# Scores in groups of four, one accumulator pair, and a longer queue of filler: the attention of a two-layer diffusion trunk, regrouped

## The chip, the cores and the metric

The kernel runs on the 8 cores of one Trainium2 chip, each core on its own share of tokens, with no exchange between them. The metric is the device time in microseconds (us) of the slowest core. Executions come in two states. In the slow one the cores of one die, or of both, run at a lower granted clock and the time is 6 to 17% longer. A ratio is the mean time of one kernel's fast runs over that of the other's of the same rounds, so it is not quite the ratio of the medians that stand beside it.

## The reference, cut to what matters

```python
# layer 0, per core: 512 context tokens (two prompts of 256) and 1281 latent tokens (1024 of its own and a halo)
h = modulate(x, g, shift, scale)                         # RMSNorm and adaLN
q, k, v, b, c, u = split(h @ w_in)                       # attention and short convolution share it
o_p = softmax([sink | q_p k_p^T / 8]) v_p                # context: 2 key blocks of 128 for each query block
o_s = softmax([sink | band of 3 key blocks | 512 cached context keys]) v    # latent: 7 key blocks
x = x + gate * (concat(o, b * dwconv3(c * u)) @ w_out)   # projection of attention and convolution
x = x + gate2 * conv_ffn(modulate(x, ...))               # then the feed-forward; layer 1 is another mixer
```

8 heads share 2 key/value heads. With 4 heads x 128 queries, one key block gives two score matmuls (one per key/value head) of 64 rows (the head dimension) by 512 columns, one exp over 128 x 1024, and two value matmuls of 512 columns. There are 13 query blocks of 128 and 70 key blocks for them, and one lone query of the halo (neighbours' tokens that a core works out for itself). SP is the prompt; S0, S1 and S2 are the latent pieces of 385, 384 and 384 tokens. A bank is one of the eight parts, 0 to 7, of the memory into which TensorE writes (PSUM). Filler is other TensorE work that is put between the key blocks.

## The kernel before

Python emits operations in program order with their dependencies; a list scheduler with a cost model then fixes each engine's order. TensorE keeps program order unless an operation isn't ready in the model. The parts that matter, cut and shortened:

```python
BK.free = [6, 7]                     # banks for filler; scores use 0, 1
ODs = ((2, 3), (4, 5))               # accumulators: two pairs, alternating by query block

def s_mm(i, u):                      # scores of one key block: two matmuls on upper and lower array half
    for hh in range(2):
        P.mm(bk(hh, 0, 512), kt(u["ky"], hh), qv(u["bl"], hh))
def s_exp(i, u):
    act_pair(pts[i % 3].whole(), 0, pair(0, 0, 512), AF.Exp, 0.125)     # then a mask on VectorE for some
def s_pv(i, u):                      # values and row sums; at a block's end normalise()
    ...
def normalise(bl):                   # 4 VectorE reads of the accumulators, Ln and Exp on ScalarE,
    ...                              # the product on GpSimd

for i in range(len(un) + 2):         # 70 key blocks
    def step(i=i):
        if i >= 2: s_pv(i - 2, un[i - 2])
        if i < len(un): s_mm(i, un[i]); s_exp(i, un[i])
    emit(step)
    acc += rate                      # n_fill / (70 - 6)
    while acc >= 1.0:                # filler: convolution, adaLN, projection of prompt and S0
        acc -= 1.0
        if fill: emit(fill.popleft())
# [cut] the lone query; then the projection of S1 and S2 beside the norm of prompt and S0; then the feed-forward
```

Of the kernel before, what the change touches and what calls it, by code (L numbers as in the profile page):

```python
# [126 lines left out]
class Prog:  # L127
# [93 lines left out]
    def cost(eng, reads, writes, is_dma):  # L221
# [7 lines left out]
        if eng == "pe":  # L229
            m = 1  # L230
            for d in reads[1].ap.shape[1:]:
                m *= d
            return max(27.0, m / 2.4 + 2.6)
# [264 lines left out]
KC = 8  # L498
# [39 lines left out]
def build():  # L538
# [40 lines left out]
    with es:  # L579
# [322 lines left out]
        IN_FLIGHT = 3.4e6  # L902
        seq = []

        def gate(n):
            n *= 512
            for op, m in reversed(seq):
                n += m
                if n > IN_FLIGHT:
                    return [op]  # L910
            return []
# [75 lines left out]
        mxS = P.tile("mxS", [128, KC, NX], BF16, O_W + 8192)  # L987
# [9 lines left out]

        def mx_(st, k):
            return mxP[:, k, :] if st.p else mxS[:, k, st.t0:st.t1]
# [4 lines left out]
        def qk_chunk(st, c):  # L1004
# [14 lines left out]
            def tail():  # L1019
# [12 lines left out]
                else:  # L1032
# [5 lines left out]
                    dst = mxS[:, c, st.t0:st.t1] if c < 4 else kS[:, st.t0:st.t1]  # L1038
# [102 lines left out]

        def norm_now(nm):
            stats(nm)
            for k in range(KC):
                nm.apply(k, E1[k], E2[k])
# [40 lines left out]
        for i in range(3):  # L1186
            pts.append(P.tile(f"pt{i}", [128, 2, 512], BF16, A_PT + 2048 * i))
# [3 lines left out]
        for c in range(4):  # L1191
            release(("q", c))

# [16 lines left out]
        for qb in range(9):  # L1210
# [5 lines left out]
            blocks.append(dict(p=False, q0=qb * 128, nq=128, keys=loc[:-1] + ks + loc[-1:]))  # L1216
        un = []
        for bl in blocks:
            for i, ky in enumerate(bl["keys"]):
                un.append(dict(bl=bl, ky=ky, first=i == 0, last=i == len(bl["keys"]) - 1))  # L1220
        BK.free = [6, 7]
        nblk = [0]
        ODs = ((2, 3), (4, 5))
# [12 lines left out]
        def s_mm(i, u):  # L1236
            for hh in range(2):
                out = bk(hh, 0, 512)
                P.mm(out.v("p (g q) -> p g q", g=4), kt(u["ky"], hh), qv(u["bl"], hh))

# [9 lines left out]
        def s_exp(i, u):  # L1250
            pt = pts[i % 3]
            act_pair(pt.whole(), 0, pair(0, 0, 512), AF.Exp, 0.125)
            mk = u["ky"][4]
            if mk is not None:
                m = tab[:, 128 + 128 * mk:256 + 128 * mk]
                pv = pt.whole().v("p h (g q) -> p (h g) q", g=4)
                P.tt("dve", pv, pv, m.w(m.ap.unsqueeze(1).to_broadcast([128, 8, 128])), ALU.mult)

        def s_pv(i, u):
            pt = pts[i % 3]  # L1260
            vb = u["ky"][3]
            kn = u["ky"][2]
            for hh in range(2):
                P.mm(bk(ODs[nblk[0] % 2][hh], 0, 512), vt[0:kn, vb, 64 * hh:64 * hh + 128], pt[0:kn, hh, :],
                     start=u["first"], stop=u["last"])
            if u["last"]:
                normalise(u["bl"])

        def normalise(bl):
            r = nrm[nblk[0] % len(nrm)]  # L1270
            OD = ODs[nblk[0] % 2]
            nblk[0] += 1
            d, nn = r["d"], r["n"]
# [29 lines left out]
        accs = [P.tile(f"acc{i}", [128, NP], F32, A_RP + 4096 + 2048 * i) for i in range(2)]  # L1303
        nA = [Norm(0, 1, SP, None, None, acc=accs[0]), Norm(0, 1, S0, None, None, acc=accs[1])]

        def oproj_a(st, nm, k):
            assert all(bl.get("done") for bl in blocks[:8])
            oproj_item(0, "we", mx_, st, nm, k, False)

        for k in range(KC):  # L1310
            for st, nm in ((SP, nA[0]), (S0, nA[1])):
                fill.append(lambda st=st, nm=nm, k=k: oproj_a(st, nm, k))
        n_fill = len(fill)
        acc = 0.0
        rate = n_fill / (len(un) - 6.0)
        for i in range(len(un) + 2):
            def step(i=i):
                if i >= 2:
# [477 lines left out]
```

## Time and profile before

| before | value | how to read it |
|---|---|---|
| median time | 1203.85 us | 16 runs, of them the fast ones 1201.9 to 1206.3 |
| PE busy | 94% of the span | TensorE is the bound almost everywhere, but a matmul at half clock is "busy" for longer (two value matmuls 1.03 us there, 0.60 otherwise) |
| first score matmul | 144.4 us | median of the eight cores |
| from it to the first feed-forward matmul | 178.3 us | median of the eight cores |
| half clock in that stretch | 27.3 us | worked out from the trace's clock records |
| from there to the last matmul | 874.5 us | PE saturated for most of it |

The stretches and the timeline are in the prediction below. In these views PE is TensorE, DVE VectorE, ACT ScalarE and POOL GpSimd; `64*128 64x512 bf16 x2` is two matmuls on 64 rows and 128 columns of the array that stream 512 columns each; brackets give the engine's idle time before and what ended it; PEclk is the granted clock. One more view of before, TensorE's waits (core 1; total us, times, longest):

```profile
PE ps L346 <- DVE pt L367: 5.6, 8, 1.1
PE ps L346 <- ACT pt L1246: 5.6, 12, 1.4
PE ps L346 <- DVE modv L367: 1.8, 2, 0.9
```

`pt` are the weights of a key block, which exp makes on ScalarE and some masks change on VectorE. "DVE pt" are value matmuls that wait for a mask. "ACT pt" are mostly score matmuls that wait until exp has read their banks: the view of the tile `pt` puts only 1.0 us of the 5.6, 3 times of 12, ahead of instructions that use `pt`. The three lines add up to 13 us, less than the 16 us for which TensorE is idle in this stretch.

### The profile page before, as it was taken

How to read it: one execution, taken by the hardware profiler on the slowest of the kernel's cores; microseconds unless marked ns; L12 is line 12 of the kernel's file. 1: busy time of each engine (PE TensorE's matmuls, PEld its weight loads, DVE VectorE, ACT ScalarE, POOL GpSimd, SP SyncE). 2: the span in 40 equal slices, each digit the busy share in tenths (PEclk: the TensorE clock that was granted, in tenths of full speed). 3: DMA queues.
4: the chain of work that ended last, by engine and by line, in shares of the span. 5: the costliest groups of instructions: out<-in, count | busy, mean ns of one | idle time of the engine just before them, and what ended most of it. 6: DMA issues, size and time to landing. Idle time of an engine off the chain costs nothing.

```text
span 1202.5 us, 21586 instructions; the slowest of 8 cores (1196.9 to 1202.5 us)
## 1 busy us (share of the span) xinstructions
PE 1129.9 (94%) x7169; PEld 625.2 (52%) x7169; DVE 748.4 (62%) x1264; ACT 622.2 (52%) x1084; POOL 480.2 (40%) x551
## 2 busy tenths in 40 slices
PE   1498999897999999999999999998999999999998
PEld 1245543332555555555555654654556566555566
DVE  3288875554689888888512522646798888882111
ACT  2276576676786555555311546445786666660000
POOL 2146521241574445454332632755764444441000
PEclk9999999997999999999999999999999999999999
DMA  9993353910404587876364570134035322225751
GB/s 178 177 207 50 52 92 52 147 29 1 71 2 73 92 140 120 140 124 124 62 111 86 92 141 1 28 53 71 12 66 101 57 51 50 49 50 116 153 128 56
DMA packets 32605, 102.28 MB, mean 85 GB/s; under 512 B 3312, under 2 KB 10096, under 8 KB 32112
## 3 DMA queue, kind: packets, MB, share of 16 engines
q0 software_dynamic: 23616, 85.21, 42.9%
q1 hardware_dynamic: 8880, 15.69, 4.0%
q8 instruction: 60, 0.98, 0.3%
q14 instruction: 49, 0.40, 0.1%
HBM read 179.27 MB, written 6.82 MB: 155 GB/s over the span
## 4 chain that ended last, share of the span: by engine, by line
PE 84%; DMA 8%; DVE 3%; issue 2%; ACT 2%; POOL 0%; SPq 0%; DVEq 0%; ACTq 0%; POOLq 0%
PE ps L346 84%; DMA xS<-xs 3%; DMA w_ada<-ada 3%; ACT pt L1246 1%; DMA xP<-xp 1%; DMA xT<-xs 1%; DVE nd L367 1%; DVE vn L388 1%; DVE pt L367 0%; DVE cvt L388 0%; ACT hS L362 0%; ACT rrs L362 0%; DVE tg L367 0%; DVE nn L394 0%; DVE xS L388 0%
## 5 line engine op out<-in xcount | busy, mean ns | idle before, releaser
L388 DVE SCALAR_TENSOR_TENSOR ft<-ps,cf,ft 128x510 f32<-128x510 f32 (+5 forms) x704 | 417.4, 630 | 67.8 <-ACT ft L362 32.9
L346 PE MATMUL ps<-hS,w_up 128*128 128x386 bf16 (+4 forms) x2112 | 334.9, 318 | 0.0
L362 ACT ACTIVATE ft<-ps,cf 128x384 f32<-128x384 f32 (+4 forms) x354 | 208.8, 592 | 130.9 <-PE ps L346 122.9
L346 PEld LDWEIGHTS ps<-hS,w_up 128*128 128x128 bf16 x2112 | 206.3, 98 | 126.6
L346 PE MATMUL ps<-hP,w_up 128*128 128x512 bf16 x704 | 160.3, 379 | 0.0
L388 DVE SCALAR_TENSOR_TENSOR xS<-ps,modv,xS 128x384 f32<-128x384 f32 (+4 forms) x96 | 56.7, 593 | 141.6 <-PE ps L346 141.0
L367 POOL TENSOR_TENSOR actT_a<-ft,ft 128x512 bf16<-128x512 f32 (+3 forms) x96 | 99.4, 1036 | 108.5 <-DVE ft L388 94.9
L346 PE MATMUL ps<-actT_a,w_dn 128*128 128x384 bf16 (+4 forms) x768 | 140.5, 333 | 0.0
L367 POOL TENSOR_TENSOR actT_b<-ft,ft 128x512 bf16<-128x512 f32 (+2 forms) x80 | 82.8, 1036 | 121.0 <-DVE ft L388 107.3
L362 ACT ACTIVATE ft<-ft 128x384 f32<-128x384 f32 (+4 forms) x178 | 95.6, 537 | 46.0 <-DVE ft L388 41.0
L346 PE MATMUL ps<-actT_b,w_dn 128*128 128x384 bf16 (+4 forms) x640 | 118.9, 333 | 0.0
L346 PEld LDWEIGHTS ps<-hP,w_up 128*128 128x128 bf16 x704 | 67.7, 98 | 75.4 <-issue 0.3
L346 PEld LDWEIGHTS ps<-actT_a,w_dn 128*128 128x128 bf16 x768 | 75.2, 98 | 54.9
L1246 ACT ACTIVATE pt<-ps 128x1024 bf16<-128x1024 f32 (+2 forms) x73 | 71.9, 985 | 35.1 <-PE ps L346 34.5
L346 PEld LDWEIGHTS ps<-actT_b,w_dn 128*128 128x128 bf16 x640 | 62.7, 98 | 45.7
L388 DVE SCALAR_TENSOR_TENSOR xP<-ps,modv,xP 128x512 f32<-128x512 f32 x32 | 24.0, 750 | 93.6 <-PE ps L346 93.5
L362 ACT ACTIVATE hS<-xS 128x384 bf16<-128x384 f32 (+3 forms) x84 | 41.7, 510 | 66.2 <-DVE xS L388 64.5
L346 PE MATMUL ps<-hS,w_cv 128*128 128x386 bf16 (+2 forms) x288 | 59.1, 333 | 4.0 <-DVE cvt L367 1.5
L400 POOL DMA_DIRECT2D w_dn<-w_dn x32 | 18.3, 572 | 103.8 <-PE ps L346 88.6
L346 PE MATMUL ps<-pt,vtok 128*128 128x512 bf16 (+2 forms) x154 | 46.9, 392 | 8.8 <-DVE pt L367 5.6
L346 PE MATMUL ps<-scb,w_ada 128*128 128x2 bf16 x768 | 25.2, 164 | 22.0 <-DMA w_ada<-ada 21.6
L362 ACT ACTIVATE hP<-xP 128x512 bf16<-128x512 f32 x28 | 17.2, 626 | 51.9 <-DVE xP L388 43.7
(183 smaller groups left out, 1337.6 us busy)
## 6 DMA issues: line engine op xcount, KB each, us to landing
w_ada<-ada POOLq DMA_DIRECT2D x48, 512.0 KB, 7.8
w_up<-w_up POOLq DMA_DIRECT2D x44, 512.0 KB, 8.2
w_dn<-w_dn POOLq DMA_DIRECT2D x32, 704.0 KB, 7.1
w_cv<-w_cv POOLq DMA_DIRECT2D x4, 768.0 KB, 9.5
xS<-xs SPq DMA_DIRECT2D x2, 1536.0 KB, 11.3
xP<-xp SPq DMA_DIRECT2D x1, 2048.0 KB, 12.0
w_we<-w_oe POOLq DMA_DIRECT2D x8, 256.0 KB, 5.1
w_u<-w_u POOLq DMA_DIRECT2D x8, 256.0 KB, 4.7
```

The costliest lines, as they stand in the source:

```text
L346: return self.add("pe", lambda e: e.matmul(out.ap, lhsT.ap, rhs.ap, start=start, stop=stop), reads=[lhsT, rhs], writes=[out])
L362: op = self.add("act", lambda e: e.activation(out.ap, in_.ap, func, **kw), reads=reads, writes=writes)
L367: return self.add(eng, lambda e: e.tensor_tensor(out.ap, in0.ap, in1.ap, op), reads=[in0, in1], writes=[out])
L388: return self.add(eng, lambda e: e.scalar_tensor_tensor(out.ap, in0.ap, sc, in1.ap, op0, op1), reads=reads, writes=[out])
L400: op = self.add(q, lambda e: e.dma_start(out.ap, in_.ap), reads=[in_], writes=[out], is_dma=True)
L1246: op = P.add("act", lambda e: e.activation(out.ap, ap, func, scale=scale), reads=r, writes=[out])
```

## The change

Its intent: pay the TensorE's change between 64-row and 128-row matmuls once per two key blocks, fill the attention to its end, and let what follows start earlier. The core of the diff:

```diff
+            if reads[0].ap.shape[0] == 64 and m > 256:     # cost model of a score matmul
+                return m / 4.8 + 53.0
...
         def norm_now(nm):
+            n0 = len(P.ops)
             stats(nm)
+            if prev:                                       # squares wait for the norm ahead
+                for o in P.ops[n0:n0 + KC]:
+                    o.deps.add(prev[-1])
+            prev.append(nm.last.idx)
...
+        blocks = [bl for two in zip(blocks[0:4], blocks[4:8]) for bl in two] + blocks[8:]
+        # steps of two key blocks; after block 7 the lone query (None)
-        ODs = ((2, 3), (4, 5))
+        OD = (4, 5)
...
+            for s, u in enumerate(steps[i]):               # four score matmuls, banks 0 to 3
+                for hh in range(2):
+                    ops.append(P.mm(bk(2 * s + hh, 0, 512) ...))
+            # the first takes over all dependencies, the others follow it at top priority
...
-        nA = [Norm(0, 1, SP, None, None, acc=accs[0]), Norm(0, 1, S0, None, None, acc=accs[1])]
+        nA = [Norm(0, 1, st, tA, rA[i], acc=accs[i]) for i, st in enumerate((SP, S0))]   # own buffers
+        fill.append(lambda: queue_apply(nA))
+        for k in range(KC):
+            fill.append(lambda k=k: oproj_a(S1, nB[0], k, 11))   # S1's projection is filler
+        KEEP = 5
-        rate = n_fill / (len(un) - 6.0)
+        rate = (len(fill) - KEEP) / float(len(steps))
```

More of the change, by code (lines that the diff above doesn't have):

```diff
@@ L900, in build @@
         SP = St(1, 0, NP)
-        IN_FLIGHT = 3.4e6
+        limit = [3.4e6]
         seq = []
@@ L908, in gate @@
                 n += m
-                if n > IN_FLIGHT:
+                if n > limit[0]:
                     return [op]
@@ L986, in build @@
         mxP = P.tile("mxP", [128, KC, NP], BF16, O_W)
-        mxS = P.tile("mxS", [128, KC, NX], BF16, O_W + 8192)
         kP = P.tile("kP", [128, NP], BF16, A_K)
@@ L996, in build @@
         nrm = []
+        ms = [P.tile("mxS", [128, KC, NX], BF16, O_W + 8192)]
         def mx_(st, k):
-            return mxP[:, k, :] if st.p else mxS[:, k, st.t0:st.t1]
+            return mxP[:, k, :] if st.p else ms[0][:, k, st.t0:st.t1]
         cos_, sin_ = (lambda a, b: cs0[:, 0, a:b]), (lambda a, b: cs0[:, 1, a:b])
@@ L1037, in tail @@
                     P.tt("pool", r["t"][:, 0, 0:n], r["t"][:, 0, 0:n], r["t"][:, 1, 0:n], ALU.add)
-                    dst = mxS[:, c, st.t0:st.t1] if c < 4 else kS[:, st.t0:st.t1]
+                    dst = ms[0][:, c, st.t0:st.t1] if c < 4 else kS[:, st.t0:st.t1]
                     P.tt("pool", dst, r["t"][:, 0, 0:n], rs, ALU.mult)
@@ L1140, in build @@
         cvt.append([P.tile(f"cvt0_{q}", [128, NP], F32, A_CV + 2048 * q) for q in range(2)])
+        prev = []
         def norm_now(nm):
+            n0 = len(P.ops)
             stats(nm)
+            if prev:
+                for o in P.ops[n0:n0 + KC]:
+                    o.deps.add(prev[-1])
+            prev.append(nm.last.idx)
             for k in range(KC):
@@ L1185, in build @@
         flush()
-        for i in range(3):
-            pts.append(P.tile(f"pt{i}", [128, 2, 512], BF16, A_PT + 2048 * i))
+        for i in range(4):
+            pts.append(P.tile(f"pt{i}", [128, 2, 512], BF16, A_PT + 2048 * i if i < 3 else A_RP))
         nrm = [dict(d=P.tile("nd0", [128, 512], F32, A_NR), n=P.tile("nn0", [128, 512], F32, A_NR + 2048))]
@@ L1192, in build @@
             release(("q", c))
+        mxS = ms[0]
         def oproj_item(l, key, src, st, nm, k, last, m=2):
@@ L1216, in build, with close @@
             blocks.append(dict(p=False, q0=qb * 128, nq=128, keys=loc[:-1] + ks + loc[-1:]))
+        blocks = [bl for two in zip(blocks[0:4], blocks[4:8]) for bl in two] + blocks[8:]
+        steps = []
         un = []
-        for bl in blocks:
+        def close():
+            if un:
+                steps.append(list(un))
+                un.clear()
+        for n, bl in enumerate(blocks):
             for i, ky in enumerate(bl["keys"]):
                 un.append(dict(bl=bl, ky=ky, first=i == 0, last=i == len(bl["keys"]) - 1))
+                if len(un) == 2:
+                    close()
+            if n == 7:
+                close()
+                steps.append(None)
+        close()
         BK.free = [6, 7]
-        nblk = [0]
-        ODs = ((2, 3), (4, 5))
+        OD = (4, 5)
+        lq = dict(p=False, q0=1152, nq=1)
+        lkeys = [("s", 1024, 128, 8), ("s", 1152, 128, 9), ("s", 1280, 1, 10)] + [("c", c * 128, 128, 15 + c) for c in range(4)]
         def kt(ky, hh):
@@ L1234, in pair @@
             return ps[0:p1, b:b + 2, lo:hi]
-        def s_mm(i, u):
-            for hh in range(2):
-                out = bk(hh, 0, 512)
-                P.mm(out.v("p (g q) -> p g q", g=4), kt(u["ky"], hh), qv(u["bl"], hh))
         def both(b, ap):
@@ L1248, in act_pair, with pt_ @@
             return op
-        def s_exp(i, u):
-            pt = pts[i % 3]
-            act_pair(pt.whole(), 0, pair(0, 0, 512), AF.Exp, 0.125)
-            mk = u["ky"][4]
-            if mk is not None:
-                m = tab[:, 128 + 128 * mk:256 + 128 * mk]
-                pv = pt.whole().v("p h (g q) -> p (h g) q", g=4)
-                P.tt("dve", pv, pv, m.w(m.ap.unsqueeze(1).to_broadcast([128, 8, 128])), ALU.mult)
-        def s_pv(i, u):
-            pt = pts[i % 3]
-            vb = u["ky"][3]
-            kn = u["ky"][2]
-            for hh in range(2):
-                P.mm(bk(ODs[nblk[0] % 2][hh], 0, 512), vt[0:kn, vb, 64 * hh:64 * hh + 128], pt[0:kn, hh, :],
-                     start=u["first"], stop=u["last"])
-            if u["last"]:
-                normalise(u["bl"])
+        def pt_(i, s):
+            return pts[(2 * i + s) % 4]
@@ new lines, in s_step @@
+        def s_step(i):
+            if steps[i] is None:
+                for hh in range(2):
+                    for n, ky in enumerate(lkeys):
+                        out = bk(hh, 4 * n, 4 * n + 4, 0, ky[2])
+                        P.mm(out.v("p (g q) -> p g q", g=4), kt(ky, hh), qv(lq, hh))
+                pt = pt_(i, 0)
+                for lo, hi, kn in ((0, 8, 128), (12, 28, 128), (8, 12, 1)):
+                    act_pair(pt[0:kn, :, lo:hi], 0, pair(0, lo, hi, kn), AF.Exp, 0.125)
+                return
+            ops = []
+            for s, u in enumerate(steps[i]):
+                for hh in range(2):
+                    out = bk(2 * s + hh, 0, 512)
+                    ops.append(P.mm(out.v("p (g q) -> p g q", g=4), kt(u["ky"], hh), qv(u["bl"], hh)))
+            own = {o.idx for o in ops}
+            for o in ops[1:]:
+                ops[0].deps.update(d for d in o.deps if d not in own)
+            for o0, o1 in zip(ops, ops[1:]):
+                o1.deps.add(o0.idx)
+                o1.prio = -1
+            for s, u in enumerate(steps[i]):
+                pt = pt_(i, s)
+                act_pair(pt.whole(), 2 * s, pair(2 * s, 0, 512), AF.Exp, 0.125)
+                mk = u["ky"][4]
+                if mk is not None:
+                    m = tab[:, 128 + 128 * mk:256 + 128 * mk]
+                    pv = pt.whole().v("p h (g q) -> p (h g) q", g=4)
+                    P.tt("dve", pv, pv, m.w(m.ap.unsqueeze(1).to_broadcast([128, 8, 128])), ALU.mult)
@@ new lines, in pv_step @@
+        def pv_step(i):
+            if steps[i] is None:
+                pt = pt_(i, 0)
+                for n, ky in enumerate(lkeys):
+                    for hh in range(2):
+                        P.mm(bk(OD[hh], 0, 4), vt[0:ky[2], ky[3], 64 * hh:64 * hh + 128], pt[0:ky[2], hh, 4 * n:4 * n + 4],
+                             start=(n == 0), stop=(n == len(lkeys) - 1))
+                normalise(lq)
+                return
+            for s, u in enumerate(steps[i]):
+                pt = pt_(i, s)
+                vb, kn = u["ky"][3], u["ky"][2]
+                for hh in range(2):
+                    P.mm(bk(OD[hh], 0, 512), vt[0:kn, vb, 64 * hh:64 * hh + 128], pt[0:kn, hh, :],
+                         start=u["first"], stop=u["last"])
+                if u["last"]:
+                    normalise(u["bl"])
@@ L1269, in normalise @@
         def normalise(bl):
-            r = nrm[nblk[0] % len(nrm)]
-            OD = ODs[nblk[0] % 2]
-            nblk[0] += 1
-            d, nn = r["d"], r["n"]
+            d, nn = nrm[0]["d"], nrm[0]["n"]
             nq = bl["nq"]
@@ L1302, in build @@
             fill.append(lambda m=m, q=q: ada_item(0, m, q))
-        accs = [P.tile(f"acc{i}", [128, NP], F32, A_RP + 4096 + 2048 * i) for i in range(2)]
-        nA = [Norm(0, 1, SP, None, None, acc=accs[0]), Norm(0, 1, S0, None, None, acc=accs[1])]
-        def oproj_a(st, nm, k):
-            assert all(bl.get("done") for bl in blocks[:8])
-            oproj_item(0, "we", mx_, st, nm, k, False)
+        accs = [P.tile(f"acc{i}", [128, NP], F32, A_RP + 2048 * (i + 1)) for i in range(2)]
+        tA = [P.tile(f"tA{i}", [128, NP], F32, A_RP + 6144 + 2048 * i) for i in range(3)]
@@ new lines, in build, with oproj_a @@
+        rA = [P.tile(f"rA{i}", [128, NP], F32, A_RP + 12288 + 2048 * i) for i in range(2)]
+        nA = [Norm(0, 1, st, tA, rA[i], acc=accs[i]) for i, st in enumerate((SP, S0))]
+        ATAIL = O_W + NFC * 1664 * 2 - 12288
+        accs.append(P.tile("acc2", [128, NP], F32, A_ES + 2048))
+        nB = [Norm(0, 1, S1, None, None, acc=accs[2]), Norm(0, 1, S2, None, None)]
+        def oproj_a(st, nm, k, upto):
+            assert all(bl.get("done") for bl in blocks[:upto])
+            oproj_item(0, "we", mx_, st, nm, k, st is S2)
@@ L1310, in build @@
         for k in range(KC):
             for st, nm in ((SP, nA[0]), (S0, nA[1])):
-                fill.append(lambda st=st, nm=nm, k=k: oproj_a(st, nm, k))
-        n_fill = len(fill)
+                fill.append(lambda st=st, nm=nm, k=k: oproj_a(st, nm, k, 8))
+        fill.append(lambda: queue_apply(nA))
[3 more added lines that the diff above has]
+        rate = (len(fill) - KEEP) / float(len(steps))
         acc = 0.0
-        rate = n_fill / (len(un) - 6.0)
@@ L1316, in build @@
-        for i in range(len(un) + 2):
+        for i in range(len(steps) + 1):
             def step(i=i):
-                if i >= 2:
-                    s_pv(i - 2, un[i - 2])
-                if i < len(un):
-                    s_mm(i, un[i])
-                    s_exp(i, un[i])
+                if i < len(steps):
+                    s_step(i)
+                if i >= 1:
+                    pv_step(i - 1)
             emit(step)
             acc += rate
-            while acc >= 1.0:
+            while acc >= 1.0 and len(fill) > KEEP:
@@ L1326, in build @@
                 acc -= 1.0
-                if fill:
-                    emit(fill.popleft())
+                emit(fill.popleft(), 1)
         while fill:
-            emit(fill.popleft())
-        bl = dict(p=False, q0=1152, nq=1)
-        keys = [("s", 1024, 128, 8), ("s", 1152, 128, 9), ("s", 1280, 1, 10)] + [("c", c * 128, 128, 15 + c) for c in range(4)]
-        pt = pts[0]
-        for hh in range(2):
-            for i, ky in enumerate(keys):
-                out = bk(hh, 4 * i, 4 * i + 4, 0, ky[2])
-                P.mm(out.v("p (g q) -> p g q", g=4), kt(ky, hh), qv(bl, hh))
@@ L1339, in build @@
-        for lo, hi, kn in ((0, 8, 128), (12, 28, 128), (8, 12, 1)):
-            act_pair(pt[0:kn, :, lo:hi], 0, pair(0, lo, hi, kn), AF.Exp, 0.125)
-        for i, ky in enumerate(keys):
-            for hh in range(2):
-                P.mm(bk(ODs[nblk[0] % 2][hh], 0, 4), vt[0:ky[2], ky[3], 64 * hh:64 * hh + 128], pt[0:ky[2], hh, 4 * i:4 * i + 4],
-                     start=(i == 0), stop=(i == len(keys) - 1))
-        normalise(bl)
-        BK.free = list(range(8))
-        nt_base = A_K
-        tA = [P.tile(f"tA{i}", [128, NP], F32, nt_base + 2048 * i) for i in range(4)]
@@ L1350, in build @@
-        rA = [P.tile(f"rA{i}", [128, NP], F32, nt_base + 8192 + 2048 * i) for i in range(2)]
-        for i, nm in enumerate(nA):
-            nm.tmps, nm.rs = tA, rA[i]
-        queue_apply(nA)
-        ATAIL = O_W + NFC * 1664 * 2 - 12288
+            emit(fill.popleft(), 2)
+        BK.free = list(range(8))
+        for k in range(KC):
+            emit(lambda: oproj_a(S2, nB[1], k, 13), 3)
         tB = [P.tile(f"tB{i}", [128, NP], F32, ATAIL + 2048 * i) for i in range(4)]
         rB = [P.tile(f"rB{i}", [128, NP], F32, ATAIL + 8192 + 2048 * i) for i in range(2)]
-        nB = [Norm(0, 1, S1, tB, rB[0]), Norm(0, 1, S2, tB, rB[1])]
@@ L1358, in build @@
-        for k in range(KC):
-            for st, nm in ((S1, nB[0]), (S2, nB[1])):
-                emit(lambda: oproj_item(0, "we", mx_, st, nm, k, st is S2), 2)
+        for i, nm in enumerate(nB):
+            nm.tmps, nm.rs = tB, rB[i]
         side_all()
```

## The prediction

> **What bounds the kernel now.** I read the page first (PE busy 94% of the span), then the busy time by stretch, which says where the other 6% and the slow clock are.
>
> ```profile
> core 1: us, PE busy (x) PEld busy (x) DVE busy (x) ACT busy (x) POOL busy (x), PEclk, DMA share, GB/s
> 0.00:95.00 95.00, 49.34 (x362) 25.97 (x363) 46.24 (x81) 43.10 (x80) 30.11 (x43) 0.98 0.91 183
> 95.00:147.00 52.00, 48.74 (x325) 28.86 (x323) 46.55 (x88) 31.98 (x69) 31.40 (x38) 0.94 0.26 40
> 147.00:222.00 75.00, 70.10 (x459) 30.19 (x459) 44.89 (x77) 51.14 (x66) 17.28 (x22) 0.98 0.55 84
> 222.00:277.50 55.50, 50.63 (x295) 19.56 (x295) 30.86 (x49) 37.25 (x49) 20.62 (x21) 0.97 0.43 68
> 277.50:299.00 21.50, 15.18 (x65) 3.54 (x64) 7.78 (x12) 12.48 (x18) 1.52 (x1) 0.68 0.00 0
> 299.00:324.50 25.50, 25.38 (x153) 14.47 (x154) 18.67 (x35) 18.57 (x35) 11.14 (x11) 0.93 0.37 63
> 324.50:760.00 435.50, 435.50 (x2843) 243.74 (x2842) 273.26 (x466) 224.01 (x394) 192.71 (x223) 1.00 0.53 92
> ```
>
> Up to 95 us the kernel loads (DMA share 0.91). From 324.5, where the first feed-forward matmul starts, PE is saturated: 435.5 busy of 435.5. The change cannot shorten that. The attention lies between, 147 to 299 us, and its last 21.5 us are poor: 65 matmuls, clock 0.68.
>
> Second, the timeline of one ordinary piece of attention and of its end:
>
> ```profile
> 170.51 0.81 PE L346 MATMUL ps<-hS,w_cv 128*128 128x384 bf16 x4
> 171.25 0.39 PE L346 MATMUL ps<-mxS,kcT 64*128 64x512 bf16 x2
> 171.58 0.60 PE L346 MATMUL ps<-pt,vtok 128*128 128x512 bf16 x2
> 172.02 1.31 PE L346 MATMUL ps<-hS,w_cv 128*128 128x384 bf16 x7
> 173.26 0.39 PE L346 MATMUL ps<-mxS,kcT 64*128 64x512 bf16 x2
> ```
>
> ```profile
> 291.45 1.03 PE L346 MATMUL ps<-pt,vtok 128*128 128x512 bf16 x2
> 291.62 1.02 ACT L1246 ACTIVATE pt<-ps 128x1024 bf16<-128x1024 f32 x1 [0.85 <-PE ps L346]
> 292.79 0.61 PE L346 MATMUL ps<-mxS,kcT 64*128 64x512 bf16 x2 [0.30 <-ACT pt L1246]
> 293.33 1.04 PE L346 MATMUL ps<-pt,vtok 128*128 128x512 bf16 x2
> 293.49 1.02 ACT L1246 ACTIVATE pt<-ps 128x1024 bf16<-128x1024 f32 x1 [0.85 <-PE ps L346]
> ```
>
> The two 64-row score matmuls of a key block (two groups of heads, upper and lower half of the array) already run side by side: two take 0.39 us together, one alone also 0.39. But they are expensive at their edges. Four 384-column matmuls at 0.163 us each end their turn at 171.16; the pair starts at 171.25, 0.09 late, and the next matmul starts 0.33 after it, though 512 columns stream in about 0.22 (the two value matmuls, 171.58 to 172.02, take 0.44). So a pair costs 0.42 us for 0.22 of work: **0.20 us of edges per pair**.
>
> The second fence is a loop between two engines with nothing to fill it: exp 1.02, release 0.15, scores, release, exp: 1.87 us per key block at half clock. The filler (convolution, adaLN, output projection) has run out at 277.3; the chain of waits names "ACT pt L1246" seven times from 279 on.
>
> **What the Trainium skill says.** "TensorEngine Tiling (Array Packing)", Key Properties: changing the tiling mode, not just the tile, drains the TensorE. The 0.09 before and the 0.11 after each pair agree. "TensorE: Matmul & The Clock Gate", Part 3 (Packing small matmuls): matmuls of different row groups run concurrently; the trace agrees (x2 in 0.39). The same page, Part 1: the array falls to half clock after an idle window of about 3.4 us; the trace shows 0.68 granted in 277.5:299 and ordinary value matmuls of 1.03 for two there instead of 0.60. "PSUM — Partial Sum Buffer", PSUM bank collisions: a bank is to be guarded by semaphores between engines, so a bank that VectorE still reads blocks the next matmul; that bears on the accumulators below, which this trace has twice and the change once.
>
> **The change, part by part.**
>
> *Pairs become fours.* Two key blocks' scores are issued as one chain of four 64-row matmuls into banks 0 to 3, so the edges are paid once per two blocks. There are 140 score matmuls of 512 columns (72 + 52 + 16 in the rows of the profile), 70 pairs. The order of blocks gives 35 + 35 key blocks, hence 36 steps, two of them single. Removed: 34 x 0.20 = 6.8 us of PE time. The new cost model's m/4.8 + 53 ns for 64 rows says the same: 4 x 0.16 = 0.64 for four, which is 0.09 + 0.22 + 0.33.
>
> *The exp loop.* Before, one loop per key block is 1.02 + 0.39 + about 0.3 for two releases = 1.7 us at full clock, against a PE turn of 1.79 per block (125 us of PE work over 70). After, two exps 2.04 + first pair 0.39 + 0.3 to 0.5 = 2.8 to 2.9 per two blocks against a PE turn of 3.3 (below). ACT gets slack it lacked: 5% before, 13% after.
>
> *More filler, and the end covered.* The lone query's block moves from the end into the middle (step 19 of 37); the output projection of S1 (8 items of 8 matmuls, 1.3 us each) joins the filler, 5 of the items being kept back to lie under the last normalisation (VectorE 4 x 0.69, ACT 2 x 0.63, POOL 1.27: about 5.5 us against 5 x 1.3 = 6.5). The filler now spreads over all steps: 24 + 12 + 16 + 1 + 3 = 56 over 37. The norm of the first two parts gets its own buffers and can start before the attention is over.
>
> PE work in the attention, 146.9 to 299.1, by counts and turns: scores 70 x 0.216 = 15.1; values 140 x 0.22 = 30.8; convolution 48 x 0.216 + 144 x 0.163 = 33.9; adaLN 192 x 0.025 = 4.8; projection 64 x 0.216 + 64 x 0.163 = 24.2; small ones 1. Sum 109.8 of 152.2 us. The missing 42.4 are 14 of pair edges, about 12 in the unfilled end (21.5 less 7.3 of work and 10 x 0.2 of edges), and about 16 of scattered waits and half-clock windows before it.
>
> After: 109.8 + 3 x 1.3 for three S1 items + 36 x 0.20 edges = 121 us with no wait at all. Before the end, the old kernel took 130.6 us for 102.1 of work plus 12.2 of edges: 1.14 times its floor. With the slack in the exp loop but the new accumulator wait (below) I take **1.12: 135.5 us**, where the old took 152.2. Behind it: 5 kept items 6.5, S2's eight 10.4, sums of squares about 1: 18 us, and 2 for the norms of the first parts, which now have about 18 us of cover at the end where they had 25. Old: 25.4. So from the start of attention to the first feed-forward matmul 177.6 becomes 155.5: **-22 us**.
>
> *Norms in order.* Each later norm's squares now wait for the former norm's 1/rms. In the old trace ACT stands 1.31 us for the last piece of x with the S1 norm's outputs queued behind it, and PE waits 2.2 us before 94.75. I give it **-1 us**: VectorE is busy 46.5 of 52 us in that stretch and will eat some.
>
> *Given back.* The accumulator has one pair of banks where it had two, and 13 blocks end with four VectorE reads (2.8 us) that the next block's first value matmul must await. A step is 3.3 us long, so it fits where a block ends at a step's end and not where the step straddles two blocks. Part of it is in the 1.12; about 1 more for the feed-forward weights arriving against a faster PE. Net **-22 us: 1204 to 1182**.
>
> **The rivals.**
>
> (a) The accumulator wait becomes the bound. For: latent blocks begin with two masked keys, so 2.8 of reads and 2 x 0.69 of masks stand in one VectorE queue before the next value matmul, more than a step; "DVE pt" already tops PE's waits there (5.6 us, 8 times). Against: VectorE is only 60% busy in 147:222, and PE has filler in banks 6 and 7. It would make 1.20 of the floor, 145 us: about 1192.
>
> (b) The end is saved, the middle was bound elsewhere: adaLN weights (PE waited for them 0.66 us once here), ACT 51 of 75 us. Then only end and part of the edges count, 12 + 3: about 1189.
>
> (c) Everything fits: waits fall to 1.06 of the floor, half-clock windows vanish. 128 us, no loss at the start of the feed-forward: about 1173.
>
> (d) The gain is given back later. Speaking against it: PE is saturated from 324.5 to 760, and all the work there follows PE in order.
>
> **Range and chances.** The two surest terms, end (12) and edges (6.8), make 19 us, 1.6%; the 2% line is 24 us, 1180. So the middle estimate lies just short of it: 1182, range 1171 to 1194. Faster by over 2%: 0.39; within 2%: 0.59; slower: 0.02, since no removed term is doubtful in sign.
>
> **What would show it.** Edges: score matmuls as x4 in one group, 0.64 us from its start less 0.09 to the start of the next matmul; if four take 0.84, the drain is paid per pair. End: no loop of exp and scores with idle PE before the S2 projection, and granted clock near 1.0 there. Accumulator: PE or the chain of waits naming "DVE nn" or "DVE nd" at block starts means rival (a). The first w_up matmul should start near 301 us instead of 324.5, and its distance to the end should stay 878 us within 3; a longer one is rival (d). The prediction is wrong if attention from its first score matmul to the first S2 projection falls outside 135 to 150 us (136 + 6.5 expected), or if the first score matmul moves by over 3 us from 146.9.

## The result, and the profile after

The changed kernel takes 1177.75 us (11 runs), a ratio of 0.9781 with a 95% interval of 0.977 to 0.9791: 2.2% faster, 26 us. It lies inside the range, 4 us below the predicted 1182 and just beyond the 2% line.

The busy time by stretch, core 1 as before, cut at its own first score matmul, last value matmul and first feed-forward matmul:

```profile
core 1: us, PE busy (x) PEld busy (x) DVE busy (x) ACT busy (x) POOL busy (x), PEclk, DMA share, GB/s
0.00:95.00 95.00, 50.30 (x367) 25.81 (x368) 45.00 (x80) 43.43 (x78) 29.37 (x42) 0.82 0.90 183
95.00:147.00 52.00, 49.53 (x341) 28.31 (x339) 46.99 (x92) 32.60 (x71) 33.05 (x39) 1.00 0.37 59
147.00:222.00 75.00, 69.60 (x532) 31.26 (x528) 51.92 (x89) 58.05 (x79) 19.54 (x25) 1.00 0.54 82
222.00:270.00 48.00, 45.99 (x267) 18.55 (x265) 30.15 (x46) 36.72 (x50) 18.81 (x19) 1.00 0.37 62
270.00:276.50 6.50, 5.71 (x33) 2.71 (x31) 4.18 (x5) 5.54 (x9) 2.27 (x3) 1.00 0.00 1
276.50:296.30 19.80, 18.54 (x112) 10.49 (x111) 18.65 (x29) 14.59 (x26) 14.01 (x15) 1.00 0.18 29
296.30:732.00 435.70, 435.70 (x2844) 243.89 (x2842) 274.67 (x469) 224.04 (x396) 192.57 (x223) 1.00 0.55 94
```

In the first 75 us of attention 532 matmuls run where 459 did (small adaLN ones included). The poor end is gone: the last stretch of attention has PE busy 5.71 of 6.5 us. The granted clock is 1.00 everywhere from 95 us on. (The 0.82 before that, for 0.98, is not the change's: in both kernels some cores run about 3 us of the first 95 at half clock and others over 30.) The first feed-forward matmul moves from 324.5 to 296.3 us, and the stretch behind it is the same, 435.7 against 435.5.

The fours in the timeline:

```profile
189.10 1.47 PE L348 MATMUL ps<-hS,w_cv 128*128 128x386 bf16 x8
190.50 0.61 PE L348 MATMUL ps<-mxP,kP 64*128 64x512 bf16 x4
191.04 1.04 PE L348 MATMUL ps<-pt,vtok 128*128 128x512 bf16 x4
```

Eight matmuls at 0.163 end their turn at 190.40; the four start 0.10 later and the value matmuls 0.54 after that. So four cost 0.64 us where two pairs cost 0.84, as foreseen.

The end of the attention:

```profile
276.39 0.38 PE L348 MATMUL ps<-pt,vtok 128*128 128x512 bf16 x1
277.39 2.77 PE L348 MATMUL ps<-mxS,w_we 128*128 128x384 bf16 x16 [0.62 <-DVE xS L390]
280.60 2.84 PE L348 MATMUL ps<-mxS,w_we 128*128 128x384 bf16 x16 [0.44 <-DVE xS L390]
```

After the last value matmul the projection runs on, 16 matmuls at a time, over the last normalisation; before, this was where exp and scores took turns.

TensorE's waits after:

```profile
PE ps L348 <- ACT pt L1269: 2.4, 6, 0.7
PE ps L348 <- DVE nn L396: 1.9, 4, 1.0
PE ps L348 <- DVE pt L369: 0.8, 1, 0.8
```

The waits named `pt` fall from 11.2 to 3.2 us. "DVE nn" is new: TensorE waits for the accumulators to be read out.

### The profile page after: what moved, and what is told of

It is laid out like the page before. It is cut to its first block, busy times and chain, and to the rows that moved or that the text cites. A ratio compares the mean times of both kernels' runs of the same rounds, so it can differ in the third digit from the quotient of the medians.

```text
span 1176.1 us, 21583 instructions; the slowest of 8 cores (1169.3 to 1176.1 us)
## 1 busy us (share of the span) xinstructions
PE 1111.2 (94%) x7162; PEld 620.6 (53%) x7162; DVE 753.3 (64%) x1265; ACT 618.3 (53%) x1084; POOL 484.9 (41%) x557
## 4 chain that ended last, share of the span: by engine, by line
PE 87%; DMA 5%; DVE 3%; issue 2%; ACT 1%; POOL 1%; DVEq 0%; SPq 0%; ACTq 0%; POOLq 0%
PE ps L348 87%; DMA w_ada<-ada 3%; DMA xS<-xs 1%; DMA xP<-xp 1%; DVE vn L390 1%; ACT hS L364 0%; DVE xS L390 0%; DVE nn L396 0%; ACT rrs L364 0%; DVE nd L369 0%; ACT pt L1269 0%; DVE hP L369 0%; DVE tg L369 0%; DVE tm L369 0%; DVE pt L369 0%
## 5 line engine op out<-in xcount | busy, mean ns | idle before, releaser
L1269 ACT ACTIVATE pt<-ps 128x1024 bf16<-128x1024 f32 (+1 forms) x73 | 68.6, 985 | 19.3 <-PE ps L348 18.9
L348 PE MATMUL ps<-pt,vtok 128*128 128x512 bf16 (+2 forms) x154 | 40.5, 360 | 4.4 <-DVE nn L396 1.9
## 6 DMA issues: line engine op xcount, KB each, us to landing
xS<-xs SPq DMA_DIRECT2D x2, 1536.0 KB, 11.2
```

Of the source, the lines that this page charges most:

```text
L348: return self.add("pe", lambda e: e.matmul(out.ap, lhsT.ap, rhs.ap, start=start, stop=stop), reads=[lhsT, rhs], writes=[out])
L1269: op = P.add("act", lambda e: e.activation(out.ap, ap, func, scale=scale), reads=r, writes=[out])
```

## The experiments

The theory after this reading: most of the gain is the attention's, by three means (edges, the exp loop, the covered end), with the norms' order a little ahead of it. The rivals are that edges were hidden in waits, that the half clock itself was the cause of the slow end, and that the single accumulator pair had become the bound. Four kernels ran in each of three calls, all with 5 rounds, each call on another chip. Two of the table's columns are medians of the eight cores in the profiled run; half clock is counted between the first score matmul and the first feed-forward one.

| kernel | median us | ratio to before (95%) | first score, us | from it to feed-forward, us | half clock, us |
|---|---|---|---|---|---|
| before | 1203.85 | 1 | 144.4 | 178.3 | 27.3 |
| changed | 1177.75 | 0.9781 (0.977 to 0.9791) | 145.8 | 149.6 | 0 |
| before_norm_order | 1200.86 | 0.9953 (0.9906 to 1.0) | 142.2 | 176.9 | 17.1 |
| after_free_norms | 1179.76 | 0.9773 (0.972 to 0.9826) | 147.2 | 150.7 | 0 |
| after_pairs | 1178.2 | 0.9768 (0.9716 to 0.9821) | 143.3 | 153.4 | 0 |
| before_s1_fill | 1199.74 | 0.994 (0.9894 to 0.9986) | 143.7 | 172.6 | 13.7 |
| before_score_banks | 1193.16 | 0.9909 (0.9893 to 0.9924) | 145.4 | 166.4 | 10.2 |
| before_s1_keep | 1199.23 | 0.9966 (0.9953 to 0.9978) | 143.8 | 174.9 | 17.1 |
| before_idle_mm | 1204.49 | 1.0014 (0.9995 to 1.0034) | 145.3 | 176.4 | 6.8 |
| after_short_reads (wrong result) | 1170.9 | 0.9726 (0.9713 to 0.9738) | 145.6 | 143.7 | 0 |
| after_again | 1177.04 | 0.9783 (0.9768 to 0.9799) | 144.9 | 149.5 | 0 |
| after_pairs_again | 1178.14 | 0.9788 (0.9775 to 0.9801) | 143.4 | 153.0 | 0 |
| before_three | 1181.38 | 0.9815 (0.9802 to 0.9828) | 140.8 | 159.5 | 3.4 |
| after_wide_reads | 1174.57 | 0.9755 (0.9742 to 0.9768) | 146.6 | 145.2 | 0 |

The first call (its four kernels are the third to sixth rows) had a noisy kernel before, 1206.09 us, hence its wide intervals. The second and third had 1203.81 and 1203.75.

### The order of the norms: added to before, removed from after

```diff
 # before_norm_order: the kernel before
+            if prev:
+                for o in P.ops[n0:n0 + KC]:
+                    o.deps.add(prev[-1])
+            prev.append(nm.last.idx)
 # after_free_norms: the changed kernel
-            if prev:
-                for o in P.ops[n0:n0 + KC]:
-                    o.deps.add(prev[-1])
```

> The kernel before with one part of the change: the squares of each later norm wait for the norm ahead of it. In the changed kernel the first score matmul stands where it stood (146.6 against 146.9 us on core 1), but 18 of the prompt's convolution matmuls, 3.9 us of TensorE work, now lie ahead of it. Theory A (the order of the norms bought that): this kernel is 3 to 5 us faster than the one before, about 1200 us. Theory B (the schedule as a whole shifted, the order has little to do with it): within 1 us of 1204. My prediction had 1 us for it.

> The changed kernel without the order of the norms. Theory A (the order is worth 3 to 5 us): about 1182 us, and fewer prompt convolution matmuls ahead of the first score matmul, 48 instead of 66. Theory B (not the order): 1177 to 1178.5.

The times alone don't settle this: 5.2 us faster with an interval that reaches no gain, and 1179.76 where the changed kernel has 1177.75, in another call. The traces do better. The same wait of TensorE (idle before it in brackets, core 1), first in the kernel before:

```profile
94.75 1.76 PE L346 MATMUL ps<-hS,w_q 128*128 128x384 bf16 x5 [2.20 <-ACT rrs L362]
```

With the order added:

```profile
93.19 0.97 PE L346 MATMUL ps<-hS,w_q 128*128 128x384 bf16 x5 [0.68 <-ACT rrs L362]
```

The changed kernel:

```profile
93.51 0.97 PE L348 MATMUL ps<-hS,w_q 128*128 128x384 bf16 x5 [0.17 <-ACT rrs L364]
```

The changed kernel without the order:

```profile
93.77 0.97 PE L348 MATMUL ps<-hS,w_q 128*128 128x384 bf16 x5 [1.20 <-ACT rrs L364]
```

So the squares of a piece that was still loading did stand in front of work that was ready. Core 1 shows this at its largest: over the eight cores the wait has a median of 0.78 us in both kernels without the order, of 0.3 in the kernel before with it and of under 0.1 in the changed one. With the order, the first score matmul comes 2.2 us sooner (144.4 to 142.2) with the same work ahead of it. Without it, it comes 1.4 us later (145.8 to 147.2) with four prompt convolution matmuls, 0.9 us, fewer ahead (62 against 66, on core 1). Both say about 2.3 us, from medians of cores that differ by 4 to 6 us within one run; that it is more than noise shows in the table, where the five kernels before without the order stand at 143.7 to 145.4 and the two with it (`before_three` is the other) at 142.2 and 140.8. Theory A had the direction right and 3 to 5 us was too much: of the 18 convolution matmuls that lie ahead of the attention in the changed kernel, 14 lie there without the order too.

### The fours taken apart

```diff
-            for s, u in enumerate(steps[i]):      # four score matmuls in a row
+            for s, u in list(enumerate(steps[i]))[part:part + 1]:   # one pair; then the value matmuls of one block
...
+                for part in range(2):
+                    if i < len(steps): s_step(i, part)
+                    if i >= 1: pv_step(i - 1, part)
```

> The changed kernel with each step's four score matmuls taken apart again: pair, value matmuls, pair, value matmuls. In the order of its TensorE instructions 54 pairs stand alone and 8 fours remain, 62 edges instead of 36. If an edge costs TensorE 0.20 us and TensorE is what bounds the attention: 26 x 0.20 = 5.2 us slower, about 1183. Rival (the exp loop bounds it, and edges are hidden in its waits): within 1.5 us of the changed kernel. Rival (splitting helps, since exp can start earlier on each pair): faster than 1177.

> The changed kernel with the fours taken apart, once more, now in the same rounds as the changed kernel, since the first time it came out at 1178.2 us where my edges asked for 1183. If fours are worth their 26 edges x 0.20: 5 us slower than the changed kernel. If the fours only shift waits (the split pairs let exp start on the first pair while the second is still to come): within 1.5 us.

> The changed kernel unaltered, so that the other three can be compared with it in the same rounds: about 0.978 of before.

In the same rounds the changed kernel takes 1177.04 and the one with pairs 1178.14 (0.9783 against 0.9788): 0.6 us by the ratios, 1.1 by the medians, and 2.0 to the first feed-forward matmul by the table's two columns (294.4 against 296.4); not 5. The edges are there:

```profile
189.68 0.39 PE L348 MATMUL ps<-mxP,kP 64*128 64x512 bf16 x2
190.00 0.60 PE L348 MATMUL ps<-pt,vtok 128*128 128x512 bf16 x2
190.54 0.39 PE L348 MATMUL ps<-mxP,kP 64*128 64x512 bf16 x2
```

Each pair again holds TensorE for 0.32 us after its start. But compare the whole attention, first score to last value matmul, on core 1. The changed kernel (run again):

```profile
142.40:271.90 129.50, 121.53 (x829) 52.67 (x828) 86.64 (x138) 100.31 (x136) 40.69 (x46) 1.00 0.45 70
```

The same with pairs:

```profile
142.30:275.10 132.80, 127.97 (x840) 55.10 (x839) 85.12 (x142) 100.74 (x137) 40.82 (x46) 1.00 0.45 72
```

PE stands idle for 8.0 us with fours (129.50 less 121.53) and for 4.8 with pairs; 11 more matmuls, prompt convolution of 2.4 us, now lie inside the attention, not ahead of it. The other seven cores say the same (8.0 to 10.9 us idle with fours, 4.8 to 7.0 with pairs). An edge removed came back as a wait. That a pair lets exp start while the other pair is still to come, where a four needs all four banks free, fits this; no run isolates it.

### Score banks

```diff
-                out = bk(hh, 0, 512)
+                out = bk(2 * (i % 2) + hh, 0, 512)
-            act_pair(pt.whole(), 0, pair(0, 0, 512), AF.Exp, 0.125)
+            act_pair(pt.whole(), 2 * (i % 2), pair(2 * (i % 2), 0, 512), AF.Exp, 0.125)
-        ODs = ((2, 3), (4, 5))
+        ODs = ((4, 5), (4, 5))
```

> The kernel before with one part of the change: scores alternate between two pairs of PSUM banks, and the accumulators give up their second pair for it. Pairs of score matmuls, filler, end and norms stay as before. Splitting the fours of the changed kernel cost next to nothing, and its waits fell by 3.7 us; that points at the banks. Theory A (one pair of score banks makes a loop of exp and scores of 1.7 us per key block, and that loop holds the attention): 6 to 12 us faster, 1192 to 1198, mostly in the unfilled end, where the loop falls from 1.87 to about 1.1 us per key block. Theory B (the loop was hidden, or the lost accumulator pair takes it back): within 3 us of before.

Theory A: 10.7 us faster (1203.81 to 1193.16), from three lines and with pairs kept (on core 1, 18 of the 140 score matmuls now run alone). The end of its attention, core 1:

```profile
282.41 0.39 PE L346 MATMUL ps<-mxS,kcT 64*128 64x512 bf16 x2
...
282.90 1.94 ACT L1246 ACTIVATE pt<-ps 128x1024 bf16<-128x1024 f32 x2 [0.64 <-PE ps L346]
283.27 0.39 PE L346 MATMUL ps<-mxS,kS 64*128 64x512 bf16 x2
```

The scores at 283.27 are made while exp, 282.90 to 284.84, still reads the other pair of banks, and two exps run back to back in 1.94 us. In the kernel before, the exps of this end each waited 0.85 us for scores. From one two exps to the next it is 2.57 us, 1.29 per key block where it was 1.87, not quite the 1.1 that I had put down. Nor does the gain lie mostly in the unfilled end. Here is the attention of both kernels on core 1, cut where the filler runs out, first before:

```profile
146.90:278.10 131.20, 121.43 (x755) 49.99 (x754) 76.16 (x126) 89.09 (x115) 37.90 (x43) 0.97 0.50 77
278.10:299.30 21.20, 14.88 (x69) 3.62 (x69) 7.63 (x13) 12.10 (x17) 1.52 (x1) 0.68 0.00 0
```

With the score banks:

```profile
146.00:274.30 128.30, 124.59 (x766) 50.90 (x766) 75.67 (x127) 91.72 (x118) 38.04 (x43) 0.99 0.49 79
274.30:289.40 15.10, 10.89 (x67) 3.93 (x66) 8.26 (x13) 10.42 (x17) 2.00 (x2) 0.89 0.01 1
```

PE's idle time falls from 9.8 to 3.7 us while there is filler, and from 6.3 to 4.2 in the end, which also gains from its clock (0.89 for 0.68). So the loop held the filled middle too. This is the largest part of those that were tested alone, and its 10.7 us are net of what the lost accumulator pair costs. The diff's words don't point to it: it came in with the fours, since a four needs four banks.

### The end covered

```diff
 # before_s1_fill
+        for k in range(KC):
+            fill.append(lambda k=k: oproj_a(S1, nB[0], k, 11))
-        rate = n_fill / (len(un) - 6.0)
+        rate = n_fill / (len(un) - 0.0)
 # before_s1_keep: also
+        KEEP = 5          # these are emitted after the lone query's normalise()
```

> The kernel before with one part of the change: the output projection of S1, 8 items of 1.3 us, becomes filler of the attention and the filler is spread to its last step; pairs, two accumulators and the lone query at the end stay. If the unfilled end with its half clock is the largest single loss, as I predicted (about 12 us in the end): 10 to 13 us faster, 1191 to 1194, and no half-clock window of over 3.5 us in the attention. Rival (the exp loop of 1.7 us per key block against a TensorE turn now of 1.9 bounds the middle as well, and the filler only moves the waits): at most 5 us faster, 1199.

> As the kernel before with the S1 projection as filler, but five of its items kept back until the lone query's block is issued, so that they lie under the last normalisation. Without that, TensorE waited 6.2 us for the last attention output and then ran 13.7 us at half clock. If the end lacked cover: 6 to 9 us faster than that kernel, so 1191 to 1194, about 0.990 of before. Rival (the lone query's own chain is the wait, as it still stands last): 2 us or less, 1198.

Both gained little, 0.6% in the noisy call and 4.6 us (1203.81 to 1199.23). I had expected 10 to 13 of the first. TensorE's wait for the last attention output, with the filler:

```profile
PE ps L346 <- POOL mxS L367: 6.2, 1, 6.2
```

and with five items kept back (its slowest core):

```profile
PE ps L346 <- POOL mxS L367: 5.9, 1, 5.9
```

Keeping items back in program order did nothing: the wait stayed, and all 64 matmuls of S1's projection again lie ahead of the last value matmul. As long as exp and scores take turns, TensorE has holes in the last key blocks, and the scheduler draws items that are ready into them. Nothing is then left for the end. (In the changed kernel 40 of the 64 are left, on core 1.)

### The half clock, cause or symptom

```diff
+            if 61 <= i < len(un):                # 4 matmuls of 384 columns that nobody reads
+                emit(lambda: idle_mm(i - 2))
```

> The kernel before with four useless matmuls of 384 columns per key block in the last nine key blocks, written to a filler bank that nobody reads; the result stays right. They add no work that counts and only keep the array busy. If the half clock is a symptom of waiting for exp: the loop goes from 1.87 to 1.7 us and the first projection runs at full clock, 2 to 4 us faster, 1200 to 1202. Rival (the half clock is itself the cause of the slow end): over 6 us faster, under 1198. If the useless work stands in the way: slower than before.

The useless matmuls did keep the clock up, 0.99 where the kernel before was granted 0.68 (columns as above):

```profile
277.50:297.00 19.50, 16.98 (x105) 7.18 (x105) 8.51 (x13) 12.15 (x17) 1.40 (x1) 0.99 0.00 1
```

The loop fell to 1.66 us per key block and the last value matmul came 2 us sooner (297.1 against 299.1, core 1), yet the kernel took 1.0014 of before. The half clock is mostly a symptom of the waits; the rival, over 6 us, falls. The test is not clean: 12 of the 36 useless matmuls ran while there still was filler and may have taken up to 2.0 us (12 x 0.163) from it, so the clock alone may be worth up to about 4 us. By the medians of the cores the first feed-forward matmul came 1.0 us sooner and what follows took 1.3 us longer (875.8 against 874.5). That may be noise: in the 14 profiles this median runs from 872.5 to 875.8.

### Three parts together

The kernel before with the score banks, the filler with five items kept back, and the norms' order, by the diffs above.

> The kernel before with three parts of the change: two pairs of score banks for the second accumulator pair, the S1 projection as filler with five items kept back, and the order of norms. No fours, no interleaved blocks, the lone query last, the first parts' norm after the attention. Alone the three gave 10.7, 4.6 and 2 to 5 us. If they add up and are the change: 18 to 22 us faster, 1182 to 1186. If end cover works only once the exp loop no longer leaves holes into which the kept items are drawn: more than the sum, about 1180. If the lone query in the middle and the early norm are what closes the end: at most 15 us, 1189.

22.4 us faster (1203.75 to 1181.38): 84% of the changed kernel's 26.7 in the same rounds. Alone they gave 10.7, 4.6 and about 2.3 (by the traces), 17.6 in sum, so together they give more. (With the 5.2 us that the noisy call gave for the order, the sum would be 20.5, so the size of the surplus is open.) The reason shows in the stretch between the last value matmul and the first feed-forward one:

```profile
283.50:299.00 15.50, 15.50 (x96) 9.19 (x95) 14.21 (x21) 11.48 (x22) 12.20 (x14) 1.00 0.27 43
```

PE is busy 15.5 of 15.5 us, where the same filler without the score banks left a wait of 5.9. The last 4.3 us to the changed kernel belong to the fours (0.6 to 2), the lone query in the middle, the interleaved blocks, the early norm, the fourth buffer for `pt` and the cost model; I didn't take these apart.

### The single accumulator pair

```diff
 # after_short_reads: the changed kernel, wrong on purpose
+                if nq == 128:                    # 128 of 512 columns
+                    P.tt("dve", d[a:z, 0:128], bk(OD[hh], 0, 128, c, y), est[c:y, 0, 0:128], ALU.add)
+                    P.copy("dve", nn[a:z, 0:128], bk(OD[hh], 0, 128, a, z))
+                    continue
 # after_wide_reads: the changed kernel, right
-                P.tt("dve", d[a:z, 0:w] ..., bk(OD[hh], 0, w, c, y) ..., e3, ALU.add)     # 64 partitions
-                P.copy("dve", nn[a:z, 0:w], bk(OD[hh], 0, w, a, z))                       # 64 partitions
-            P.act(d[:, 0:w], d[:, 0:w], AF.Ln)
+                P.tt("dve", sm[:, 0:w] ..., bk(OD[hh], 0, w) ..., sinks[hh][:, :, 0:nq], ALU.add)  # 128; zero sink on values
+                P.act(d[a:z, 0:w], sm[c:y, 0:w], AF.Ln)
```

> The changed kernel with VectorE reading only 128 of the accumulators' 512 columns at each block's end; its result is wrong on purpose. It gives the single accumulator pair back 4 x 0.69 less 4 x about 0.2 = 2.0 us sooner at 13 block ends and takes 26 us of work from VectorE. The trace shows TensorE waiting about 2 us in all for these reads. If that is all the single pair costs: 1 to 3 us faster than the changed kernel, about 1176. Rival (the pair is the bound, as in my rival a): 6 us or more, under 1172.

> The changed kernel with the accumulators read in two VectorE operations of 128 partitions per block in place of four of 64; the logarithm then takes two ScalarE operations of 64 partitions in place of one of 128, and the product two on GpSimd. The result stays right. The short reads, wrong in their result, gave 6.9 us for 26 us less of VectorE work. This takes 13 x 2 x 0.69 = 18 us from VectorE and releases the banks 1.4 us sooner, and gives ScalarE 13 x 0.63 = 8 us more. If VectorE and the single pair are the bound: 2 to 5 us faster than the changed kernel. If ScalarE is as near its bound: no gain, or up to 3 us slower.

Less reading gives 6.1 to 6.9 us (1170.9 against 1177.04 and 1177.75, other calls), three times what the waits named "DVE nn" add up to, and inside the rival's mark, 6 us or more and under 1172. The whole attention of the short reads, core 1:

```profile
142.60:266.20 123.60, 120.76 (x830) 53.43 (x831) 64.44 (x139) 100.38 (x137) 40.03 (x45) 1.00 0.47 72
```

VectorE falls from 86.64 to 64.44 us and PE's idle time from 8.0 to 2.8. That tells that reading the accumulators costs this much; the sooner release and VectorE's lighter load came together and are not told apart.

The version with two wide reads keeps the result right and takes 1174.57 us, against 1177.04 for the changed kernel in the same rounds: 2.5 us faster, 0.9755 of before, and the fastest correct kernel. (The intervals of the two ratios just touch.) ScalarE pays for it:

```profile
147.70:272.80 125.10, 120.28 (x829) 53.16 (x829) 66.46 (x113) 108.17 (x150) 56.79 (x58) 1.00 0.45 73
```

ACT is at 108.17 of 125.1 us, 86%, where the changed kernel had 100.31 of 129.5, 77%. TensorE is idle for 4.8 us of this stretch (125.1 less 120.28), so little more is to be had from its waits here.

## Why the prediction was right or wrong

Its total was right, 1182 for 1178, and for the stretch behind the attention the working was. Its split of the gain was not: three terms were mis-sized, and that their errors offset each other was luck. Neither of its two signs of being wrong came: on core 1 the first score matmul stands at 146.6 us for 146.9, and the first S2 projection follows about 138 us later (135 to 150). But the first feed-forward matmul came at 296.3, not near 301.

- **"Removed: 34 x 0.20 = 6.8 us of PE time."** Count and cost per edge were measured as written (34 fours, 0.64 us). What failed is the step from TensorE's time to the kernel's: called one of the "two surest terms", it is worth 0.6 to 2 us, by the 26 edges that were put back. Putting them back gave TensorE 5.2 us of edges (26 x 0.20) and took 3.2 us of waits away.
- **"ACT gets slack it lacked: 5% before, 13% after."** The mechanism was named, but it got no us of its own and was dissolved in a factor of 1.12. It measures 10.7 us by itself, with pairs and the old filler, and three quarters of the idle time that it saves lie before the end. I read the loop of exp and scores as a matter of the unfilled end; a turn of 1.79 us against a loop of 1.7 should have been read as two bounds on top of each other.
- **"end (12)".** As a part alone it is 4.6 us, since a loop with holes draws the filler in. With the score banks the end closes. The two can't be priced apart, as my sum did.
- **Norms in order, "-1 us".** About 2.3 us. Small, in the right direction, by the mechanism described (squares of a loading piece in front of ready work).
- **"1.12: 135.5 us" and "18 us, and 2".** On core 1 the attention took 129.9 us. The scheduler moved 18 prompt convolution matmuls, 3.9 us, ahead of it, so its work was 109.8, not 113.7, and its floor with 36 edges 117.0: a factor of 1.11. The stretch behind took 19.7 us for the 20 predicted. So of the 6 us by which 155.5 missed the measured 149.7, 4.4 are that shift (3.9 x 1.12). I had not seen it. (The prediction's 102.1 us of work before the end should read 102.5, 109.8 less 7.3; its factor of 1.14 stays.)
- **Rival (a), the accumulator wait,** did not bring the 1192 that it foretold, but its mechanism is there: "DVE nn" appears, as it said, and without most of the reads the changed kernel is 6.1 to 6.9 us faster; 2.5 of that were had with a right result. **Rival (c)** foresaw that the half-clock windows would vanish (27.3 us to 0); the time lies between it and the main line. **Rival (d)** fell: 876.8 us from the first feed-forward matmul to the end of core 1's span, for 878.0 before.
- **The chances.** It held "within 2%" the likelier, 0.59; what came is the 0.39, over 2% faster. The line lay 2 us from the middle of the forecast.

Open: what lone query, interleaving, early norm, fourth buffer and cost model give each (4.3 us with the fours), and how much of the order's 2.3 us is the wait that was shown.

## What to carry to other kernels

When two engines hand one buffer to and fro, compare the loop's length with the bound engine's turn: where they are as close as here (1.7 against 1.79 us), a second buffer may be worth more than any shortening of either side, and it can even be worth giving up double buffering elsewhere. TensorE time saved counts only where TensorE doesn't then wait: undo the saving on the finished kernel before crediting it. Filler kept for the end stays there only if the stretch ahead of it has no holes.

## What the Trainium skill lacked or had wrong

- "TensorEngine Tiling (Array Packing)", Key Properties, says that a change of tiling mode drains the TensorE, without a length, and no other page gives one for it. Here a group of 64-row matmuls starts 0.09 to 0.10 us late and the next matmul after it about as much: 0.20 us per group, for two (0.42 in all) and for four (0.64) alike.
- "TensorE: Matmul & The Clock Gate", the section "HAM oscillation — how this bites in real kernels", gives as the rule that there be no idle gaps over about 3.4 us. (The page's next section tells of a kernel whose frequent short idles did the same, without their length or share.) In the kernel before, core 1 ran 13.7 us at half clock (first fence) though no gap of TensorE near its start was over 1.4 us (second fence, idle in brackets). In the 3.4 us ahead of the fall (279.1 to 282.5) TensorE was busy for 1.33, so here a low share of work was enough:

```profile
282.40:296.10 13.70, 10.85 (x28) 1.81 (x28) 4.05 (x6) 7.91 (x9) 1.52 (x1) 0.50 0.00 0
```

```profile
280.87 0.39 PE L346 MATMUL ps<-mxS,kS 64*128 64x512 bf16 x2 [1.37 <-ACT pt L1246]
282.53 0.61 PE L346 MATMUL ps<-mxS,kS 64*128 64x512 bf16 x2 [0.73 <-ACT pt L1246]
```

- The same page, Terms, puts the penalty of throttled time at that time x (1 - K/N), here half, and no page says what a warm clock is worth when TensorE waits for another engine. Useless matmuls raised the granted clock of the end from 0.68 to 0.99 and cut the half clock from 27.3 to 6.8 us, which would be 10 us by that rule (an estimate); the time stayed at 1.0014 of before.
